# HGRN2 block products: seven levels and the diagonal in one run per unit, into two PSUM banks

## The chip, the cores and the metric

The kernel runs on one core of one Trainium2 chip. The metric is the device time of one execution in microseconds; lower is better. A core has a matrix engine (TensorE, PE in the profile, with its weight loads as PEld), a vector engine (VectorE, DVE), a scalar engine (ScalarE, ACT), a general engine (GpSimd, POOL), and SyncE (SP), whose queue issues the transfers here. The engines work from queues of their own and wait for each other through semaphores. TensorE writes its products into PSUM, of which a bank holds 512 float32 columns for 128 partitions; the other engines read them from there.

## What is computed

The reference is a decoder trunk of two layers over 1024 tokens of width 1024. Layer 0 mixes tokens with gated DeltaNet heads and a short convolution, layer 1 with HGRN2 heads and dilated sliding-window attention; a SwiGLU network follows each. The change is in the HGRN2 heads of layer 1 (four heads, key and value width 128), for which the reference says:

```python
def hgrn2_recurrence(q, k, v, log_f):
    '''S_t = diag(f_t) S_{t-1} + k_t v_t^T with k_t = 1 - f_t, o_t = S_t^T q_t, chunkwise.'''
    bcum = jnp.cumsum(lf, axis=3)
    def step(state, inp):
        q_c, k_c, v_c, b_c = inp
        decay = masked_exp(causal, b_c[:, :, :, None, :] - b_c[:, :, None, :, :])
        attn = jnp.einsum('bhtsd,bhsd->bhts', decay * q_c[:, :, :, None, :], k_c)
        o = (jnp.einsum('bhts,bhse->bhte', attn, v_c)
             + jnp.einsum('bhtd,bhde->bhte', q_c * jnp.exp(b_c), state))
        b_last = b_c[:, :, -1:, :]
        state = (state * jnp.exp(b_last[:, :, 0, :, None])
                 + jnp.einsum('bhsd,bhse->bhde', k_c * jnp.exp(b_last - b_c), v_c))
        return state, o
```

The weights of `attn` between positions t and s carry a decay for every one of the 128 key channels, so they are not one matrix product. The kernel splits the triangle of (s, t) pairs of a 128-token chunk into levels: at block size 1, 2, 4, ... 64, the pairs whose earlier position lies in the first half of a block of twice the size and whose later one lies in the second half. Within a level the decay can be written as a factor of the earlier position times a factor of the later one, both taken from the middle of the block, and the level is a matrix product of two decayed operands. The diagonal needs no decay.

## The kernel before

Tokens are held in two halves of 512. Dense products are made in three terms per tile, of a high and a low part of each operand (`mm3`, lines 125 to 137): one weight load and one matmul of up to 512 columns each. PSUM is one pool with three tags, each a rotation of banks: `psg` (two banks), `psu` (three) and `psm` (three).

In `mixer_cd`, three things are woven together. The outer order is that of the dense projections: `hgrn_v` for the values of the HGRN2 heads, `swa_v` for those of the attention, `hgrn_gates` for the output gates. Between their pieces they call `tick`, which earns credits (2.2 per unit of cost for the HGRN2 chain) and spends each on one step of `hg_chain` or of the attention's generator `local`. `chain` runs `hgrn(h, half, states)` for eight units, the two halves of heads 0 to 3; each `yield` in `hgrn` ends a step. The loop at line 1988 forces the chain on, without any projection between its steps, until three units are done, and the loop at line 2149 forces it until the unit whose gate comes next is done. Outside a block with an order written out by hand, which this stage has not, a planner orders the instructions of each engine ahead of time: by program order as the priority, taking what is ready by its own estimates. So the order of the code is a preference here, not the order that runs.

A unit's work in `hgrn`, with the lines of the code before:

- lines 2008 to 2012 load `b` (the cumulated log decay), `kk` and `q` of this unit or of the next one
- `decayed(bs)`, lines 2014 to 2032, makes the operand of one level: VectorE subtracts the reference row, ScalarE takes the exponential, VectorE multiplies with `kk` (first halves) and `q` (second halves). At block size 1, GpSimd copies `kk`. The result lies in a buffer with tag `m` (three of them) or, at sizes 8 and 64, `e4` (three, shared with later tiles of the unit)
- `blocks(od, a, x)`, lines 2034 to 2040, makes 16 products of 32 by 32 positions for one level, each with 128 rows of contraction and 32 columns of the array at a tile position; a float32 product is two matmul instructions in the trace
- the first run, lines 2048 to 2055: one `psg` bank takes the diagonal (`kk` with `q`) and levels 1, 2 and 4, 64 products, 128 instructions; VectorE masks the diagonal into `ac` and takes in each level with a masked copy (`take`, line 2043)
- the operands of levels 8, 16, 32 and 64 are made at line 2056, and two steps later comes the second run, lines 2059 to 2071: another `psg` bank, levels 8 and 16 by `blocks`, level 32 with 8 products and level 64 with 4 products of 64 columns, 88 instructions
- lines 2072 to 2081 bring both into `attn`: VectorE takes in levels 8 and 16, ScalarE copies levels 32 and 64, GpSimd copies `ac`
- lines 2084 to 2092 decay `q` and `kk` in place (`kk` for the state); line 2097 transposes `kk` into a `psg` bank; lines 2103 to 2116 update the states; lines 2118 to 2134 make and normalize the output; lines 2137 to 2142 transpose it and store it

Ten `yield`s stand in a unit. `hgrn_gates` (lines 2145 to 2157) reads the stored outputs back, makes `xg` (tag `xg`, two buffers) and stores the gated result. `out_proj` loads the mixer's outputs in `cin` tiles, in layer 1 into three buffers with tag `m`, for half 0 all eight and for half 1 two of them; the others go into other tags.

## Time and profile before

| | |
|---|---|
| time before, median of 3 runs | 2527.8 us (2527.16 to 2528.48) |
| span of the profiled execution | 2525.5 us |
| busy in the span: TensorE | 2508.2 us (99%) |
| busy: weight loads | 2086.1 us (83%) |
| busy: VectorE | 1683.2 us (67%) |
| busy: ScalarE | 1079.6 us (43%) |
| busy: GpSimd | 662.9 us (26%) |
| HBM read and written | 304.74 MB and 144.26 MB, 178 GB/s over the span |
| mean granted TensorE clock | 0.998 |

The span runs from the first to the last instruction of one profiled execution; the times of the runs are 2.3 us above it at the median. An engine's busy time is the union of its instructions' durations. Matmuls are pipelined: one starts before the last one has ended, so how close TensorE is to its limit is read from the distance between starts. An idle engine that nobody waits for costs nothing. Line numbers (L2039) are those of the kernel; a helper such as `blocks` has one line for all its callers, and is told apart by the tiles that it reads.

### The profile page before, as it was taken

How to read it: one execution, taken by the hardware profiler on the slowest of the kernel's cores; microseconds unless marked ns; L12 is line 12 of the kernel's file. 1: busy time of each engine (PE TensorE's matmuls, PEld its weight loads, DVE VectorE, ACT ScalarE, POOL GpSimd, SP SyncE). 2: the span in 40 equal slices, each digit the busy share in tenths (PEclk: the TensorE clock that was granted, in tenths of full speed). 3: DMA queues.
4: the chain of work that ended last, by engine and by line, in shares of the span. 5: the costliest groups of instructions: out<-in, count | busy, mean ns of one | idle time of the engine just before them, and what ended most of it. 6: DMA issues, size and time to landing. Idle time of an engine off the chain costs nothing. (4 is left out here: it accounts for less than half of the span.)

```text
span 2525.5 us, 37470 instructions
## 1 busy us (share of the span) xinstructions
PE 2508.2 (99%) x13955; PEld 2086.1 (83%) x13955; DVE 1683.2 (67%) x2812; ACT 1079.6 (43%) x1829; POOL 662.9 (26%) x591
## 2 busy tenths in 40 slices
PE   9999999999999999999999999999999999999998
PEld 7888888888888888887888889888888888888887
DVE  8887786685656565567788756666668565656554
ACT  5432113353333344334677535556635333334442
POOL 1321111343333300033466401000134343340001
PEclk9999999999999999999999999999999999999999
DMA  4535447325556688533444444577732555668753
GB/s 156 163 121 175 124 156 253 119 89 186 184 192 209 208 296 293 185 134 134 131 153 138 159 152 146 153 204 220 250 132 88 188 183 192 206 211 293 273 175 125
DMA packets 281454, 451.48 MB, mean 179 GB/s; under 512 B 49176, under 2 KB 137784, under 8 KB 281016
## 3 DMA queue, kind: packets, MB, share of 16 engines
q1 hardware_dynamic: 280984, 448.57, 53.3%
q8 instruction: 109, 1.79, 0.3%
q14 instruction: 73, 0.60, 0.1%
q10 hardware_dynamic: 288, 0.52, 0.1%
HBM read 304.74 MB, written 144.26 MB: 178 GB/s over the span
## 5 line engine op out<-in xcount | busy, mean ns | idle before, releaser
L103 DVE TENSOR_TENSOR w<-raw,w 128x1024 fp32r<-128x1024 f32 (+1 forms) x327 | 386.0, 1182 | 136.2 <-ACT w L102 134.3
L102 ACT CAST w<-raw 128x1024 fp32r<-128x1024 f32 (+1 forms) x327 | 309.4, 952 | 286.3 <-PE psu L137 143.2
L135 PE MATMUL psu<-hnh,w 128*128 128x512 f32 x772 | 309.0, 400 | 0.0
L137 PE MATMUL psu<-hnh,w 128*128 128x512 f32 x772 | 301.7, 391 | 0.0
L136 PE MATMUL psu<-hnl,w 128*128 128x512 f32 x772 | 301.4, 390 | 0.0
L196 POOL TENSOR_TENSOR acc<-acc,sq 128x512 f32<-128x512 f32 x52 | 78.8, 1515 | 439.4 <-ACT sq L192 435.1
L335 POOL TENSOR_TENSOR ws<-raw 128x512 f32<-128x512 f32 x54 | 70.7, 1310 | 412.2 <-DMA raw<-in_dram 317.7
L135 PEld LDWEIGHTS psu<-hnh,w 128*128 128x128 f32 x772 | 145.2, 188 | 30.8 <-ACT sq L192 0.8
L137 PEld LDWEIGHTS psu<-hnh,w 128*128 128x128 f32 x772 | 145.0, 188 | 31.1
L136 PEld LDWEIGHTS psu<-hnl,w 128*128 128x128 f32 x772 | 145.3, 188 | 28.1
L103 DVE TENSOR_TENSOR w<-ws,w 128x1024 fp32r<-128x1024 f32 x51 | 68.3, 1339 | 120.8 <-ACT w L102 120.8
L103 DVE TENSOR_TENSOR hidq<-hr,hidq 128x1024 fp32r<-128x1024 f32 x72 | 82.4, 1146 | 76.9 <-ACT hidq L102 76.8
L102 ACT CAST hidq<-hr 128x1024 fp32r<-128x1024 f32 x72 | 70.2, 979 | 102.0 <-DMA hr<-ts 59.6
L135 PE MATMUL psm<-hidq,w 128*128 128x512 f32 (+1 forms) x275 | 106.2, 386 | 0.0
L136 PE MATMUL psm<-hidq,w 128*128 128x512 f32 (+1 forms) x275 | 105.9, 385 | 0.0
L137 PE MATMUL psm<-hidq,w 128*128 128x512 f32 (+1 forms) x275 | 105.9, 385 | 0.0
L341 POOL TENSOR_TENSOR raw<-raw,ws 128x512 f32<-128x512 f32 x51 | 79.7, 1563 | 57.5 <-DVE w L103 56.2
L426 POOL TENSOR_TENSOR hid<-hid,c 128x512 f32<-128x512 f32 x44 | 62.1, 1410 | 124.1 <-ACT hid L425 123.6
L135 PE MATMUL psu<-t4h,w 128*128 128x512 f32 x240 | 93.6, 390 | 0.0
L136 PE MATMUL psu<-t4l,w 128*128 128x512 f32 x240 | 93.5, 389 | 0.0
L137 PE MATMUL psu<-t4h,w 128*128 128x512 f32 x240 | 93.5, 389 | 0.0
L137 PE MATMUL psu<-t3h,w 128*128 128x512 f32 x240 | 93.5, 389 | 0.0
(546 smaller groups left out, 6761.9 us busy)
## 6 DMA issues: line engine op xcount, KB each, us to landing
raw<-in_dram SPq DMA_DIRECT2D x225, 512.0 KB, 4.3
sd<-in_dram SPq DMA_DIRECT2D x44, 512.0 KB, 4.1
hid<-hid SPq DMA_DIRECT2D x88, 256.0 KB, 3.0
sd<-sd SPq DMA_DIRECT2D x44, 512.0 KB, 3.3
hr<-ts SPq DMA_DIRECT2D x40, 512.0 KB, 4.4
raw<-sd SPq DMA_DIRECT2D x40, 512.0 KB, 4.5
qk<-z SPq DMA_DIRECT2D x52, 256.0 KB, 3.8
hd<-h SPq DMA_DIRECT2D x48, 256.0 KB, 2.7
```

Of the source, the lines that this page charges most:

```text
L102: S.copy(hi, src)
L103: eng.tensor_tensor(lo, src, hi.bitcast(F32), op=SUB)
L135: T.matmul(o, lh, rh, start=first and i == 0, stop=False, **kw)
L136: T.matmul(o, lh, rl, start=False, stop=False, **kw)
L137: T.matmul(o, ll, rh, start=False, stop=last and i == n - 1, **kw)
L196: (eng or G).tensor_tensor(a, a, q, op=ADD)
L335: G.tensor_tensor(s[:, HT:], b[:, :HT], b[:, HT:], op=ADD)
L341: G.tensor_tensor(a[:, HT:], a[:, HT:], s[:, :HT], op=SUB)
L426: G.tensor_tensor(h, h, self.c22.pop(f), op=MULT)
```

## The change

All operands are made first, in two steps (levels 1, 2, 4; then 8, 16, 32, 64). Three `yield`s, not four, stand ahead of the products. Then one run makes all 108 products: the diagonal and levels 1, 2 and 4 into one `psg` bank, `ol`, and levels 8 to 64 into the other, `od`. All masking and copying out follows. To hold all five of its operands at once, tag `m` has five buffers in place of three; the two of `xg` are given up, and `xg` uses tag `m`. The `cin` tiles of `out_proj` in layer 1 rotate through the five as well; layer 0 keeps four.

```diff
@@ out_proj
-                f = hp.tile([P, HT], F32, tag="m", name="cin", bufs=4 - layer)
+                f = hp.tile([P, HT], F32, tag="m", name="cin", bufs=4 + layer)
@@ hgrn, decayed
-                    m = hl("m", bufs=3) if bs not in (8, 64) else hl("e4", (4, P), 3).rearrange("p c t -> p (c t)")
+                    m = hl("m", bufs=5) if bs not in (8, 64) else hl("e4", (4, P), 3).rearrange("p c t -> p (c t)")
@@ hgrn
-                ms = [decayed(1), decayed(2), decayed(4)]
+                small = [decayed(1), decayed(2), decayed(4)]
+                yield
+                ms = [decayed(8), decayed(16), decayed(32), decayed(64)]
                 yield
                 yield
                 ac = hl("ac", (4, 32))
-                od = psg()
-                blocks(od[:, 0:P], kk, q)
-                for i, m in enumerate(ms):
-                    blocks(od[:, (i + 1) * P:(i + 2) * P], m, m)
-                V.tensor_tensor(ac, c4(od[:, 0:P]), dia32[:, None, :].to_broadcast([P, 4, 32]), op=MULT)
-                for i in range(3):
-                    take(i, od[:, (i + 1) * P:(i + 2) * P])
-                ms = [decayed(8), decayed(16), decayed(32), decayed(64)]
-                yield
-                yield
+                ol = psg()
+                blocks(ol[:, 0:P], kk, q)
+                for i, m in enumerate(small):
+                    blocks(ol[:, (i + 1) * P:(i + 2) * P], m, m)
                 od = psg()
                 for i in range(2):
                     blocks(od[:, i * P:(i + 1) * P], ms[i], ms[i])
...
+                V.tensor_tensor(ac, c4(ol[:, 0:P]), dia32[:, None, :].to_broadcast([P, 4, 32]), op=MULT)
+                for i in range(3):
+                    take(i, ol[:, (i + 1) * P:(i + 2) * P])
                 for i in range(2):
                     take(i + 3, od[:, i * P:(i + 1) * P])
@@ hgrn_gates
-                        xg = hl("xg", bufs=2)
+                        xg = hl("m", bufs=5)
```

## The prediction

> **What bounds the kernel now.** I read the page's busy shares first, then the same shares of the stage that the change touches, then the waits of TensorE there, and last the timelines of TensorE and VectorE around two of the runs. A unit below is one head and half of the HGRN2 loop, numbered 0 to 7 as `chain` takes them.

> ```profile
> span 2525.5 us, 37470 instructions
> ...
> PE 2508.2 (99%) x13955; PEld 2086.1 (83%) x13955; DVE 1683.2 (67%) x2812; ACT 1079.6 (43%) x1829; POOL 662.9 (26%) x591
> ...
> PEclk9999999999999999999999999999999999999999
> ```

> TensorE is busy 99% of the span, at a granted clock that the row of slices shows at the top tenth throughout. The eight units run from about 1430 to 1810 us, and the windows of that stretch add up to the same picture:

> ```profile
> sum 380.00, PE 375.52 PEld 324.72 DVE 248.97 ACT 208.33 POOL 31.09; mean PE 93.88 PEld 81.18 DVE 62.24 ACT 52.08 POOL 7.77
> ```

> TensorE is busy 375.5 of 380 us and VectorE 249. So a gain must come from one of two places: from fewer microseconds of TensorE's own stream, or from these waits, which are all that the trace gives it in the stretch:

> ```profile
> PE psu L136 <- issue: 1.4, 1, 1.4
> PE psm L2276 <- ACT sc L2271: 1.1, 1, 1.1
> PE psu L135 <- ACT vt L1991: 0.5, 1, 0.5
> PE psg L2139 <- DVE e L2134: 0.3, 1, 0.3
> PE psm L2313 <- DVE pt L2296: 0.3, 1, 0.3
> PE psm L2241 <- DVE stat L2249: 0.2, 1, 0.2
> PE psm L2313 <- DVE dp L2284: 0.2, 1, 0.2
> ```

> They sum to 4.0 us, 0.16% of the span. A wait that VectorE, ScalarE or GpSimd loses matters only if it ends up in this list.

> **The change part by part.** First, what TensorE pays for a run by itself. This is its timeline around the first run of unit 0 (columns: start, duration, line, output and inputs, shape, count; the duration of a merged row reaches from the first start to the last end), and the durations of one block product:

> ```profile
> 1453.40 0.28 PE L136 MATMUL psu<-w,b22h 128*128 128x256 f32 x1
> 1453.52 0.28 PE L137 MATMUL psu<-w,b22l 128*128 128x256 f32 x1
> 1453.73 0.46 PE L2039 MATMUL psg<-q,kk 128*32 128x32 f32 x32
> 1454.00 1.05 PE L2039 MATMUL psg<-m 128*32 128x32 f32 x96
> 1454.98 0.39 PE L135 MATMUL psu<-w,t1h 128*128 128x256 f32 x1
> 1455.20 0.28 PE L136 MATMUL psu<-w,t1h 128*128 128x256 f32 x1
> 1455.32 0.28 PE L137 MATMUL psu<-w,t1l 128*128 128x256 f32 x1
> ...
> L2039 PE MATMUL psg<-m x1024: 189/197/216, 1454.0 to 1719.1; 128*32 128x32 f32 x171
> ```

> Read starts, not durations, since matmuls overlap. Full-array matmuls of 256 columns start every 0.12 us. The run's first product starts 0.21 us after the last of them, so going in costs 0.09. The last product ends at 1455.05 and takes 0.197, so it started at 1454.85; the next full-array matmul starts 0.13 later, where products follow each other at 0.01: going out costs 0.12. The second full-array matmul then starts 0.22 behind the first, not 0.12: another 0.10. The edges of one run are 0.09 + 0.12 + 0.10 = 0.31 us, beside 1454.85 - 1453.73 = 1.12 us for its 128 instructions.

> The change moves those 128 instructions, none fewer, to the head of the unit's second run. That run now has this form (unit 1):

> ```profile
> 1494.41 0.39 PE L137 MATMUL psu<-w,b22l 128*128 128x512 f32 x1
> 1494.72 0.46 PE L2039 MATMUL psg<-e 128*32 128x32 f32 x32
> 1495.00 0.49 PE L2039 MATMUL psg<-m 128*32 128x32 f32 x32
> 1495.34 0.45 PE L2065 MATMUL psg<-m 128*32 128x32 f32 x16
> 1495.71 0.45 PE L2070 MATMUL psg<-e 128*64 128x64 f32 x8
> 1496.09 0.66 PE L2097 MATMUL psg<-cf,kk 128*128 128x128 f32 x4
> 1496.50 0.48 PE L135 MATMUL psu<-w,t1h 128*128 128x512 f32 x1
> ```

> The two groups of 32 products take 0.28 and 0.34 us, much as the 0.27 of the first 32 in unit 0. Passing from a group of level masks to the next one, in another tile, shows no edge of 0.31, and I assume the same where the run passes from bank `ol` to bank `od`. One run's edges go per unit; the second run's own stay. That this holds for all units is seen in the windows around the eight first runs:

> ```profile
> 1453.00:1456.00 3.00, 1.32 (x128) 1.21 (x128) 1.00 1.00 347
> ...
> sum 24.00, PE 10.71 PEld 9.81; mean PE 1.34 PEld 1.23
> ```

> Eight runs of 128 instructions, 10.71 us in all, 1.32 in the first: none is split. **Removed: 8 x 0.31 = 2.5 us** of TensorE's stream. This is the term I trust.

> Second, what used to lie between the two runs. `kk` is read by the first run (its diagonal product), and overwritten at line 2092 for the transposes at line 2097. So in the kernel before, that update could be made while TensorE was still on its way to the second run:

> ```profile
> 1488.61 0.43 DVE L2023 TENSOR_TENSOR m<-b 128x256 f32<-128x256 f32 x1 [6.30 <-PE psg L2039]
> ...
> 1490.19 0.28 DVE L2053 TENSOR_TENSOR ac<-psg,cf 128x128 f32<-128x128 f32 x1
> ...
> 1490.72 0.30 DVE L2043 COPY_PREDICATED ac<-ci,psg 128x128 f32<-128x128 int32 x1
> ...
> 1492.91 0.69 DVE L2087 TENSOR_TENSOR q<-q,t 128x512 f32<-128x512 f32 x1
> ...
> 1493.85 0.68 DVE L2092 TENSOR_TENSOR kk<-kk,b 128x512 f32<-128x512 f32 x1
> ```

> In unit 1 `kk` was ready at 1494.53, before the second run began at 1494.72, and so the transposes stand right behind that run at 1496.09. They do so in two more units:

> ```profile
> 1602.88 0.45 PE L2070 MATMUL psg<-e 128*64 128x64 f32 x8
> 1603.26 0.55 PE L2097 MATMUL psg<-cf,kk 128*128 128x128 f32 x3
> ...
> 1681.49 0.45 PE L2070 MATMUL psg<-e 128*64 128x64 f32 x8
> 1681.87 0.66 PE L2097 MATMUL psg<-cf,kk 128*128 128x128 f32 x4
> ```

> With one run, the update waits for that run in every unit. VectorE then has, between the run and the transposes, the diagonal (0.28), up to five masked copies (5 x 0.30), `q` (0.69) and `kk` (0.68): 3.15 us. The transposes also need the bank of `ol` back, which the same copies free. The subtraction and exponential of `b` need no run and can stand ahead of it. Queued on VectorE behind these are the next unit's masks and the splits of weights; on TensorE nothing has to queue behind the transposes, because the planner that orders this stage can put a projection's matmuls ahead of them. By the credits of `tick`, a step leaves at least 24 matmuls of 256 columns, or 18 of 512, behind the run: 24 x 0.12 = 2.9 us or more, about the 3.15 us that are needed. What it costs where the cover falls short is bounded by nothing (as in the five units where the transposes already stand apart) and by the full 3.15 us in three units, 9.5 us. I take 0.3 us twice, the price of the nearest row, line 2139's transposes waiting on VectorE for the same kind of update: +0.6. For transposes that lose their place beside the run and now leave two more changes of shape, I take +0.1 over the three units: the row behind them, 1496.50, starts 0.41 after four transposes, so hardly an edge is seen there.

> Third, the steps. A unit yields nine times in place of ten. In the kernel before, line 1988 forces five steps of units 2 and 3 with no projection between them, among them the normalization that ends in line 2139's wait (0.3 us, above); counted through with nine steps, that loop forces only the step that closes unit 2. So -0.3. The chain ends a step or two sooner, which buys nothing: it ends long before the stage does,

> ```profile
> L2139 PE MATMUL psg<-cf,e x32: 269/272/330, 1477.7 to 1749.1; 128*128 128x128 f32 x32
> ```

> with its last transposes at 1749.1 of 1810, and TensorE's work is the same.

> Fourth, the buffers. `m` has five places, so the masks of levels 16 and 32 no longer wait for the first run:

> ```profile
> DVE m L2023 <- PE psg L2039: 23.2, 9, 6.3
> ```

> That is 23.2 us of VectorE in nine waits, 6.3 us of it the first row of the VectorE timeline above. VectorE's queue is in order, so weight splits and score reductions stood behind them; but TensorE's list shows only 0.7 us of waits on VectorE besides line 2139's (0.3 + 0.2 + 0.2). I count 0 and keep the 0.7 for the range. `xg` shares these five places, as do the `cin` tiles of `out_proj`, which had three; more loads can be under way, hidden behind a TensorE that waits for none of them in this stretch. Cost 0; if an `xg` came late, its projection would hold one of three `psu` banks. The SyncE queue carries the same transfers, none added.

> **Sum:** -2.5 + 0.6 + 0.1 - 0.3 = -2.1 us. Against the profiled execution's span that is 2525.5 - 2.1 = 2523.4; the median of the three runs, 2527.8, lies 2.3 above that span, so the forecast is 2525.7, or -0.08%. A measurement of this kernel can tell about 0.2%, 5.1 us, from no change; so this is "the same".

> **The rivals.**

> *The transposes' wait eats the gain.* The edges go, but waits of about 0.3 us appear in all eight units (2.4), or the planner keeps two runs by putting other matmuls between `ol`'s products, whose masks come first, and `od`'s. Either gives 2527.5, within a few tenths. For it: in unit 1 the update of `kk` had from 1488.61, where the first run released VectorE, to the second run at 1494.72, and loses those 6.1 us. Against it: TensorE has other matmuls to take.

> *Slower: evacuation on the path.* Both `psg` banks are taken until VectorE has emptied them, and the transposes need the first. Place: lines 2053 to 2097 in units 1, 4 and 6, where they now follow the run at once. Price: 3 x 3.15 = 9.5 us, less 2.5 and with the 0.1: +7.1, 2534.9. It decides when such waits pass 7.6 us, 2.5 in each of the three. Against it speaks the planner, and that VectorE is idle a third of the stretch (249 of 380 us busy). [...]

> *Faster.* All the 4.0 us of TensorE's waits go, since VectorE is rid of 23.2 us of waiting and every later instruction stands at another place: -2.5 - 4.0 = -6.5, 2521.3. Against it: 1.4 us of them are put down to nothing that the profile shows and 1.6 to ScalarE.

> **How the numbers follow.** The forecast (2523.5 to 2527) has 0.52; the eaten gain (2527 to 2529) 0.25; the slower rival 0.11; the faster one 0.12. The first two are within 0.2%: same 0.77, faster 0.12, slower 0.11. The range joins the first two and reaches about half way into the others: 2521.5 to 2530.5.

> **What would show it.** After the change, eight runs of 216 instructions at lines 2039 to 2070's successors, each with one pair of edges; TensorE's busy time about 2.5 us shorter; VectorE's wait of masks on block products gone; the transposes some 3 us behind the run in every unit. It is wrong if TensorE's list shows waits at the transposes, if the products stand in more than eight runs, or if the stages behind line 1288 change by more than 1 us, since a schedule that is shifted as a whole can gain or lose waits that have nothing to do with these products.

## The result: 1% slower, all of it in the stage of the eight units

The changed kernel takes 2552.0 us (median of 4 runs, 2549.3 to 2553.8) against 2527.5 us, a ratio of 1.010 with a 95% interval of 1.0087 to 1.0112. I forecast 2525.7 and a range up to 2530.5. The profiled execution has a span of 2547.5 us, 22.0 more than before. Its page looks harmless:

```profile
span 2547.5 us, 37466 instructions
...
PE 2513.0 (99%) x13955; PEld 2092.2 (82%) x13955; DVE 1686.2 (66%) x2812; ACT 1081.7 (42%) x1829; POOL 666.3 (26%) x591
```

The same number of matmuls, 99% busy as before. Windows over three stretches (columns: stretch, its length, busy time and count of each engine, granted clock, DMA share, GB/s) say where the 22 us are; first the kernel before, then the changed one:

```profile
0.00:1430.00 1430.00, 1425.51 (x6864) 1176.39 (x6864) 1005.53 (x1504) 597.32 (x926) 435.27 (x397) 1.00 0.51 171
1430.00:1808.00 378.00, 373.52 (x3896) 323.07 (x3897) 248.97 (x791) 208.33 (x552) 31.09 (x55) 1.00 0.60 183
1808.00:2525.00 717.00, 709.14 (x3198) 586.68 (x3196) 428.68 (x518) 273.93 (x352) 196.56 (x139) 1.00 0.56 192
```

```profile
0.00:1430.00 1430.00, 1424.48 (x6864) 1175.72 (x6864) 1006.73 (x1504) 597.41 (x926) 436.63 (x397) 1.00 0.52 171
1430.00:1830.00 400.00, 379.31 (x3895) 329.83 (x3896) 249.09 (x789) 208.90 (x549) 31.55 (x55) 0.98 0.56 171
1830.00:2547.00 717.00, 709.23 (x3198) 586.65 (x3196) 430.40 (x520) 275.43 (x354) 198.12 (x139) 1.00 0.57 192
```

The stretches were chosen so that the counts of matmuls agree. Ahead of 1430 us and behind the stage nothing has moved. The stage itself does 3895 matmuls in 400 us that took 378. TensorE's idle time in it has grown by 16.2 us (20.7 against 4.5) and its busy time by 5.8. The stage has lost some of its clock: 0.98 of 400 us is about 8 us of full speed that was not granted. The waits of TensorE in that stage name the rest:

```profile
PE psg L2039 <- issue: 13.8, 5, 4.6
PE psg L2066 <- issue: 2.2, 1, 2.2
PE psg L2096 <- DVE ac L2043: 1.6, 2, 0.8
PE psg L135 <- ACT hnh L102: 1.4, 1, 1.4
```

16.0 us, in six pauses, stand at the block products themselves (L2066 is the product of level 64), and the releaser is "issue": TensorE waited for no semaphore that the profile shows. The transposes' wait for VectorE, on which my slower rival was built, is the third row: 1.6 us. The timeline of the first unit shows a pause in the middle of the run:

```profile
1456.51 0.28 PE L137 MATMUL psu<-w,b22l 128*128 128x256 f32 x1
1456.72 0.46 PE L2039 MATMUL psg<-q,kk 128*32 128x32 f32 x32
...
1458.17 0.33 PE L2039 MATMUL psg<-m 128*32 128x32 f32 x14
1463.06 0.45 PE L2039 MATMUL psg<-m 128*32 128x32 f32 x17 [4.55 <-issue]
...
1464.48 0.58 PE L135 MATMUL psu<-w,t1h 128*128 128x256 f32 x1
1464.86 0.42 PE L136 MATMUL psu<-w,t1h 128*128 128x256 f32 x1
1465.07 0.41 PE L137 MATMUL psu<-w,t1l 128*128 128x256 f32 x1
```

175 matmuls go out in 1.6 us, then nothing for 4.75 us (start to start), in the midst of one level's products, whose operand is one tile that is there or not as a whole. Behind the pause the full-array matmuls start 0.21 us apart where they took 0.12: the granted clock is 0.50 in the window from 1462.80 to 1466.20 us. The windows around another pause show that by themselves:

```profile
1603.00:1607.00 4.00, 0.62 (x67) 0.52 (x58) 3.25 (x10) 1.68 (x3) 0.25 (x1) 0.89 0.89 177
1607.00:1611.00 4.00, 3.92 (x37) 3.45 (x37) 0.86 (x5) 0.66 (x3) 0.00 (x0) 0.50 0.02 7
```

What TensorE lacks is its own instructions. The table of DMA queues has two of the kind "instruction", one of them with 109 packets:

```profile
q8 instruction: 109, 1.79, 0.3%
```

1.79 MB in 109 packets is 16.4 KB each, and TensorE's 13955 matmuls and 13955 weight loads over 109 packets come to 256 instructions to a packet. The count goes with the instructions in the experiments below: 117 packets with 8 x 256 more of them, 113 with 8 x 128 more, 103 with 8 x 192 fewer. A float32 product is two weight loads and two matmuls here: the 64 products of unit 0's first run stand in the window from 1453 to 1456 us of the kernel before as 128 of each. The prediction counted the matmuls alone (128 and 88 a run); with the weight loads the runs before had 256 and 176 instructions, and the merged one has 432. In the window from 1448.5 to 1460.6 us of the changed kernel no packet of that queue moves; in the next one, 1460.6 to 1461.8, there is one (columns: queue and kind, packets, MB, share):

```profile
q1 hardware_dynamic: 160, 0.39, 84.1%
q8 instruction: 1, 0.02, 5.2%
```

By the records of the packets it starts at 1460.69 and lands at 1461.68, and TensorE goes on at 1463.06. By the same records the other five agree: TensorE goes on 1.2 to 1.5 us after a packet of that queue has landed.

**The theory, then,** is my reading of these traces: TensorE's instructions come in blocks of 256. By the starts above, a stream of full-array matmuls uses one up in an estimated 15 us or more (128 pairs of a weight load and a matmul at 0.12 us); the 128 pairs of unit 0's first run were through in 1.12 us. A run that crosses one block's edge lives on what has been brought in ahead; one that crosses two stands still until the next has come. Its rivals are my own slower case (both banks and `kk` held until VectorE is done) and the shared `m` buffers.

### The profile page after: what moved, and what is told of

The parts are those of the page before. It is cut to its first block, busy times and chain, and to the rows that moved or that the text cites. A ratio compares the mean times of both kernels' runs of the same rounds, so it can differ in the third digit from the quotient of the medians.

```text
span 2547.5 us, 37466 instructions
## 1 busy us (share of the span) xinstructions
PE 2513.0 (99%) x13955; PEld 2092.2 (82%) x13955; DVE 1686.2 (66%) x2812; ACT 1081.7 (42%) x1829; POOL 666.3 (26%) x591
## 3 DMA queue, kind: packets, MB, share of 16 engines
q8 instruction: 109, 1.79, 0.3%
## 4 chain that ended last, share of the span: by engine, by line
PE 49%; DVE 3%; issue 1%; ACT 1%; DMA 0%; SPq 0%; DVEq 0%; POOLq 0%; POOL 0%; ACTq 0%
PE psu L135 8%; PE psu L137 8%; PE psu L136 8%; PE psg L135 3%; PE psg L137 3%; PE psg L136 3%; PE psm L135 2%; PE psm L137 2%; PE psm L136 2%; PE psm L2312 1%; PE psu L130 1%; PE psu L132 1%; PE psu L129 1%; PE psg L2039 1%; PE psm L2237 0%
## 5 line engine op out<-in xcount | busy, mean ns | idle before, releaser
L102 ACT CAST w<-raw 128x1024 fp32r<-128x1024 f32 (+1 forms) x327 | 309.4, 952 | 277.0 <-PE psu L137 147.1
L135 PE MATMUL psu<-hnh,w 128*128 128x512 f32 x772 | 308.8, 400 | 0.0
L137 PE MATMUL psu<-hnh,w 128*128 128x512 f32 x772 | 301.5, 391 | 0.0
L136 PE MATMUL psu<-hnl,w 128*128 128x512 f32 x772 | 301.2, 390 | 0.0
L135 PEld LDWEIGHTS psu<-hnh,w 128*128 128x128 f32 x772 | 145.1, 188 | 31.0 <-ACT sq L192 0.8
L137 PEld LDWEIGHTS psu<-hnh,w 128*128 128x128 f32 x772 | 144.9, 188 | 31.0
L136 PEld LDWEIGHTS psu<-hnl,w 128*128 128x128 f32 x772 | 145.2, 188 | 28.2
L102 ACT CAST hidq<-hr 128x1024 fp32r<-128x1024 f32 x72 | 70.2, 979 | 104.6 <-DMA hr<-ts 64.6
L135 PE MATMUL psm<-hidq,w 128*128 128x512 f32 (+1 forms) x275 | 106.1, 386 | 0.0
L136 PE MATMUL psm<-hidq,w 128*128 128x512 f32 (+1 forms) x275 | 105.8, 385 | 0.0
L137 PE MATMUL psm<-hidq,w 128*128 128x512 f32 (+1 forms) x275 | 105.8, 385 | 0.0
L135 PE MATMUL psu<-t4h,w 128*128 128x512 f32 x240 | 93.5, 390 | 0.0
L137 PE MATMUL psu<-t4h,w 128*128 128x512 f32 x240 | 93.4, 389 | 0.0
L136 PE MATMUL psu<-t4l,w 128*128 128x512 f32 x240 | 93.4, 389 | 0.0
L137 PE MATMUL psu<-t3h,w 128*128 128x512 f32 x240 | 93.4, 389 | 0.0
```

Of the source, the lines that this page charges most:

```text
L102: S.copy(hi, src)
L135: T.matmul(o, lh, rh, start=first and i == 0, stop=False, **kw)
L136: T.matmul(o, lh, rl, start=False, stop=False, **kw)
L137: T.matmul(o, ll, rh, start=False, stop=last and i == n - 1, **kw)
```

## The experiments

**The run cut again, all else as changed.** One more step end, so that projections lie between the products into `ol` and those into `od`:

```diff
                 for i, m in enumerate(small):
                     blocks(ol[:, (i + 1) * P:(i + 2) * P], m, m)
+                yield
                 od = psg()
```

> The changed kernel with one more step end between the products into ol and those into od, so that projections lie between them again: runs of 128 and 88 matmuls (256 and 176 instructions with their weight loads); operands made first, five m buffers, xg in m and the late evacuation all stay. Theory of the instruction fetch (TensorE goes through a run faster than its instructions are brought in, 256 at a time, and the merged run crosses two such blocks): no pause over 1 us inside a run, granted clock 1.00 in the stage from 1430 us, time 2524 to 2530. Theory of the evacuation (both psg banks and kk held by the run until VectorE is done): about half of the loss stays, 2535 to 2548. Theory of the buffers (xg and cin in the five m places): 2545 to 2553, unchanged.

Measured: 2531.5 us, ratio 1.0022 (1.0013 to 1.0031), 1.5 us over the range that the fetch theory gave. Four fifths of the loss are gone. Of the rest its list of waits names 3.7 us:

```profile
PE psg L2039 <- issue: 3.7, 3, 1.8
```

Three pauses are left, in the units where the parts are nearest: two where the second part begins 4.3 and 5.0 us after the first, and unit 5, where the planner put them side by side again:

```profile
1639.91 0.46 PE L2039 MATMUL psg<-q,kk 128*32 128x32 f32 x32
1640.19 1.07 PE L2039 MATMUL psg<-m 128*32 128x32 f32 x96
1641.11 0.33 PE L2039 MATMUL psg<-e 128*32 128x32 f32 x16
1642.35 0.30 PE L2039 MATMUL psg<-e 128*32 128x32 f32 x13 [0.91 <-issue]
```

The five units whose parts lie 5.8 to 8.7 us apart have none. So the expectation "no pause" failed for a reason that fits the theory: it is the distance of the products, not a step in the code, that counts.

**The buffers alone.** The kernel before with `m` at five, `xg` in `m` and `cin` rotating through five:

```diff
-                f = hp.tile([P, HT], F32, tag="m", name="cin", bufs=4 - layer)
+                f = hp.tile([P, HT], F32, tag="m", name="cin", bufs=4 + layer)
-                    m = hl("m", bufs=3) if bs not in (8, 64) else ...
+                    m = hl("m", bufs=5) if bs not in (8, 64) else ...
-                        xg = hl("xg", bufs=2)
+                        xg = hl("m", bufs=5)
```

> The kernel before with the three edits of buffers alone (m with five, xg in m, cin rotating through five); two runs as before. Instruction fetch: 2524 to 2529. Evacuation: the same, 2524 to 2529. Buffers: 2545 to 2553.

Measured: 2527.1 us, ratio 1.0004 (0.9994 to 1.0014), no different from the kernel before within the interval. The buffers are not it. They leave one small trace, the row "PE psg L135 <- ACT hnh L102: 1.4, 1, 1.4" that the changed kernel's list of waits has above: it stands here too, and in every kernel with this edit (with 1.2 us in one of them), and in none without it. That is `out_proj` waiting for the split of a `cin` tile.

**The run made longer, nothing else.** In the kernel before, the first run's products are issued twice into the same bank:

```diff
-                blocks(od[:, 0:P], kk, q)
-                for i, m in enumerate(ms):
-                    blocks(od[:, (i + 1) * P:(i + 2) * P], m, m)
+                for _ in range(2):
+                    blocks(od[:, 0:P], kk, q)
+                    for i, m in enumerate(ms):
+                        blocks(od[:, (i + 1) * P:(i + 2) * P], m, m)
```

> The kernel before with the products of its first run issued twice into the same bank (256 matmuls, 512 instructions); nothing else is changed, no wait, operand or evacuation is added. Extra products: 8 x 1.1 = 9 us. Instruction fetch: the run crosses two blocks of 256 every time, so pauses of 0.7 to 5 us in at least six of the eight first runs, half the granted clock behind the long ones, time 2550 to 2575. Evacuation and buffers: the extra products alone, 2535 to 2539, no pause over 1 us inside a run.

Measured: 2577.6 us (one run), 52 above the 2525.9 of the kernel before beside it, of which the products themselves are 9. That is 2.6 us over the upper end of what the fetch theory gave, and 39 over its rivals'. All eight first runs pause, up to 5.9 us:

```profile
PE psg L2039 <- issue: 27.7, 8, 5.9
```

This is the plainest of the experiments: no operand, bank, buffer or wait is new, and the second half of the products needs nothing that the first had not. The eight runs of 512 instructions have pauses of 27.7 us in all, where the eight of 432 had 16.0.

**The same run with fewer instructions.** The changed kernel without the products of levels 1, 2 and 4 and their masked copies:

```diff
                 blocks(ol[:, 0:P], kk, q)
-                for i, m in enumerate(small):
-                    blocks(ol[:, (i + 1) * P:(i + 2) * P], m, m)
...
-                for i in range(3):
-                    take(i, ol[:, (i + 1) * P:(i + 2) * P])
```

> The changed kernel without the products and masked copies of levels 1, 2 and 4 (their operands are still made; the output is not the reference's): one run of 120 matmuls, 240 instructions, behind the same operands, into the same two banks. Left out: 8 x 96 matmuls at 9 ns, 7 us. Instruction fetch: no pause over 1 us inside a run, clock 1.00, 2514 to 2522. Evacuation: the update of kk still follows the run and both banks are still taken, three copies of five are gone; most of the loss stays, 2533 to 2546. Buffers: 2538 to 2546.

Measured: 2524.0 us (one run), 2 us above the upper end of what the fetch theory gave and 9 below the lower end of its nearest rival. No run has a pause; that of unit 0 goes through in 1.7 us:

```profile
1457.41 0.46 PE L2039 MATMUL psg<-q,kk 128*32 128x32 f32 x32
...
1458.69 0.45 PE L2064 MATMUL psg<-e 128*64 128x64 f32 x8
1459.08 0.39 PE L135 MATMUL psu<-w,t1h 128*128 128x256 f32 x1
```

The microseconds over the forecast stand beside waits of another kind: the state update (L2109, L2111) and `kk` (L2087) come late for TensorE. I take it that the chain's steps follow the run more closely when it has no pause; that was not taken apart.

```profile
PE psg L2118 <- DVE st L2109: 2.1, 1, 2.1
PE psg L2118 <- DVE st L2111: 1.9, 1, 1.9
...
PE psg L2092 <- DVE kk L2087: 0.8, 3, 0.4
```

**A length in between.** The kernel before with the diagonal and level 1 issued twice, 384 instructions:

```diff
+                for n in (2, 4):
+                    blocks(od[:, 0:P], kk, q)
+                    for i, m in enumerate(ms[:n - 1]):
+                        blocks(od[:, (i + 1) * P:(i + 2) * P], m, m)
```

> The kernel before with half of its first run's products issued twice (diagonal and level 1), so that the run has 192 matmuls, 384 instructions; nothing else is changed. Extra products: 8 x 64 matmuls at 9 ns, 4.6 us. Instruction fetch: between the one block of 256 that the run before crosses and the two that 512 cross; 384 instructions reach a second block's edge from half of the possible starting points, so 3 to 5 of the eight first runs pause by 0.7 us or more; 2540 to 2555. Evacuation: 2530 to 2533, no pause.

Measured: 2549.3 us (one run). Four pauses that nothing releases, as expected; but only one lies inside a run, and three just behind one, at the next thing that TensorE had to do:

```profile
PE psg L2039 <- issue: 3.9, 1, 3.9
PE psu L136 <- issue: 3.4, 1, 3.4
PE psm L2263 <- issue: 2.9, 1, 2.9
...
PE psu L135 <- issue: 1.4, 1, 1.4
```

Of the 22.5 us over the kernel before, the added products are 4.6 and the four pauses 11.6; the rest is nearly all clock, which by its record stood at half for 13.65 us.

**Where the edges fall.** This can be counted in the traces. Take TensorE's records in order of start: matmuls, weight loads and the few instructions of its queue. In the nine kernels of this document 25 of its pauses are put down to "issue" and last over 0.25 us. Each of the 25 ends at a place in this order that leaves 193 when it is divided by 256: 14529 is 56 x 256 + 193 in unit 0 of the changed kernel, 20417 is 79 x 256 + 193 behind the first run of unit 7 in the kernel before. By the theory these places are the edges of blocks; in these traces no pause of this kind ends anywhere else. The six merged runs that pause hold two such places each and stop at the second; the two that go through, units 2 and 6, hold one. Of the eight runs of 384 instructions one has its second edge inside and three have it 12 to 23 instructions behind, and there the four pauses are; the other four have no second edge so near.

Counted alike for eight first runs, the pauses inside a run and close behind one are: 240 instructions, none and none; 256 in the kernel before, none and one; 384, one and three; 432, six and none; 512, eight and one.

**The two parts further apart.** The changed kernel with two step ends in place of one between `ol` and `od`.

```diff
                     blocks(ol[:, (i + 1) * P:(i + 2) * P], m, m)
+                yield
+                yield
```

> The changed kernel with two step ends, not one, between the products into ol and those into od; one lets the planner put the two parts 4 to 5 us apart or, in one unit, side by side. Instruction fetch: the parts lie 6 us or more apart, no pause over 1 us, clock 1.00; the time is that of the kernel with the buffers alone, 2525 to 2529. Evacuation (what is left of it once the fetch is out of the way: one late evacuation, kk updated behind it): 3 us or more above the kernel before, 2529 to 2533.

Measured: 2530.9 us, ratio 1.0017 (1.0008 to 1.0026). No pause is left in any run, and the time is still 4.2 us above the 2526.8 of the kernel before beside it. So the second expectation is the one that holds for what is left, in its size: the arrangement costs some 4 us without the pauses. The largest of its waits are these:

```profile
PE psg L135 <- ACT hnh L102: 1.2, 1, 1.2
PE psm L2294 <- ACT sc L2251: 1.2, 1, 1.2
```

The first is the `cin` wait of the buffers. The others, 1.2 us and less each, are ScalarE and VectorE coming late here and there; which part of the edit causes each was not taken apart. Part of the 4 us is clock again. The profiled execution has one period of half clock, 3.41 us from 1797.51, right behind the `cin` wait and another wait for the same split; and over the eleven executions the two at a mean clock of 0.999 took 2528.6 and 2528.7 us, the four at 0.997 between 2530.5 and 2533.1.

**The edges by themselves.** The kernel before with its first run cut into two, eight more entries and exits:

```diff
                 for i, m in enumerate(ms):
+                    if i == 1:
+                        yield
+                        yield
                     blocks(od[:, (i + 1) * P:(i + 2) * P], m, m)
```

> The kernel before with its first run cut in two by two step ends (diagonal and level 1, then levels 2 and 4): three runs per unit in place of two, eight more entries and exits in all, same instructions. If the edges of a run cost the 0.31 us that I read off the timeline: 2.5 us more, 2527 to 2531, and in the trace an entry of about 0.09, an exit of about 0.12 and a late second matmul of about 0.10 us for every additional run. If runs had no edges of their own: no change. Instruction fetch: no pause, runs are shorter.

Measured: 2532.7 us, ratio 1.0022 (1.0012 to 1.0032), 3 to 8 us more, and 1.7 over the range that was given. An added run of 64 matmuls in unit 0:

```profile
1459.09 0.28 PE L137 MATMUL psu<-w,b22l 128*128 128x256 f32 x1
1459.30 0.76 PE L2039 MATMUL psg<-m 128*32 128x32 f32 x64
1459.99 0.50 PE L135 MATMUL psu<-w,hnh 128*128 128x512 f32 x1
1460.33 0.39 PE L136 MATMUL psu<-w,hnh 128*128 128x512 f32 x1
```

Going in costs 0.21 less the usual 0.12, so 0.09; the second full-array matmul starts 0.34 behind the first in place of 0.23, another 0.11. In this run the edges are as I read them. The time moved by more than their 2.5 us, and beside them stand 2.5 us of waits for the normalization of the output, where the kernel before had 0.3; the unit now has twelve steps (that these cause the waits was not shown):

```profile
PE psg L2142 <- DVE e L2137: 2.5, 3, 1.1
```

No version that makes all the products is faster than the kernel before; the one with the buffers alone is level with it.

## Why the prediction was wrong

**The step that failed** is the one on the moved instructions: "The change moves those 128 instructions, none fewer, to the head of the unit's second run", with the assumption that passing from `ol` to `od` costs nothing because the passage between groups of masks costs nothing. I priced a run as its edges plus 9 ns for each matmul, whatever its length. It has a third term, which in the changed kernel was zero in the two runs that met one block's edge and 0.7 to 4.75 us in the six that met a second one. There that term is 16.0 us of pauses by the list of waits, and some 8 us of clock, nearly all of it behind them. TensorE's busy time, which was to fall by 2.5 us, rose by 4.8 (2513.0 against 2508.2), and by 5.8 in the stage: in the main the lost clock less the edges that were saved. With the 16.2 us by which its idle time in the stage grew, that is the 22.0 us of the span. None of my rivals had this term.

**The sign was there and was read past.** "PE psu L136 <- issue: 1.4" heads the list of waits in the prediction; I counted it as something that "nothing that the profile shows" explains, and kept it for the faster rival. It stands right behind the first run of unit 7 and is this same term: the run's first edge lies 13 instructions into it and the second 14 behind its end. A packet of the instruction queue lands at 1710.90, and TensorE goes on at 1712.29, 1.4 us later.

**The edges, 2.5 us saved.** Right in kind and perhaps a little large. The added runs of the last experiment confirm about 0.31 us a run. But a merged run can have inner edges of its own. In unit 6 of the changed kernel, which has no pause:

```profile
1683.00 0.39 PE L137 MATMUL psu<-w,hnl 128*128 128x512 f32 x1
1683.32 0.46 PE L2039 MATMUL psg<-q,kk 128*32 128x32 f32 x32
...
1685.57 0.45 PE L2066 MATMUL psg<-e 128*64 128x64 f32 x8
1685.95 0.44 PE L2275 MATMUL psm<-cf,sc 128*128 128x128 f32 x2
```

From the last full-array matmul to the next thing it takes 2.95 us. Before, the two runs of that unit took 1.57 (1671.61 to 1673.18) and 1.75 (1680.12 to 1681.87), together 3.32; less one spacing of 0.23 that belongs to a full-array matmul, and with up to 0.10 for the late second one that these starts do not hold, the saving is 0.14 to 0.24 us, or 1.1 to 1.9 us for eight such units. In unit 2, the other run without a pause, the same sum gives 0.32 us (2.88 against 1.57 and 1.75, less a spacing of 0.12), which is the 0.31 of the prediction.

**The transposes behind the run, +0.6.** The two waits are there, with 1.6 us in place of 0.6, but the mechanism is not quite the one that I gave: the waits are for the masked copies that free the bank of `ol`. `kk` is updated while the run still stands in its pause, as VectorE's timeline of unit 0 shows:

```profile
1457.86 0.92 DVE L2091 TENSOR_TENSOR kk<-kk,b 128x512 f32<-128x512 f32 x1
```

It waits for the diagonal's products only, and the run lasts until 1464.5, so the cover that I thought lost was not. In all eight units `kk` is done before the run ends. The slower rival was built on 9.5 us of such waits, and they were not seen.

**The buffers at 0.** Nearly: 1.4 us in `out_proj`, where I saw only loads hidden behind TensorE.

**The steps and the rest of the arrangement, -0.3 and 0.** Wrong in sign: with the pauses taken away, 4.2 us remain over the kernel before. Some 1.7 of them are half clock in the profiled execution. The wait of VectorE's mask operands on the first run (23.2 us) is gone, as foretold. But VectorE is not rid of the wait: the update of `q` now stands in its place, in all eight units,

```profile
DVE q L2086 <- PE psg L2039: 29.9, 8, 6.1
```

and TensorE gained nothing from the exchange.

What stays open: why a block takes 2 us in one unit and 6 in another. In the changed kernel the packet started sooner where less data moved: 1.4 us after the start of the run in unit 1 (share 0.37 over its first 4 us) and 4.0 in unit 0 (0.95). Of the other four paused runs three fall into this order (just ahead of the run in unit 3, 2.2 us after its start in unit 7, 2.6 in unit 5, at shares of 0.19, 0.73 and 0.87) and unit 4 does not (2.5 us, with the largest share). That speaks for the data transfers standing in its way; it was not tried.

## What to carry to other kernels

Count the instructions of a burst, not only its time. Here TensorE went through 256 instructions in 1.12 us, and the six merged runs that paused went on with the next block 2.0 to 6.3 us after their starts. So bursts of short matmuls are to be kept to about one block, with some 6 us of long ones in between. In the two cut kernels that sufficed: parts whose starts lay 5.6 us or more apart had no pause. It is no bound, for in unit 0 of the doubled run TensorE got its next block only 7.2 us after it had passed the edge before. A wait that is put down to nothing ("issue") and stands in or behind a burst of tiny instructions is to be suspected as a shortage of instructions: all 25 of over 0.25 us in these traces ended at the edge of a block. Two bursts that look like waste may be what hides the fetch: here the kernel with two runs a unit took 2527.5 us, and that with one 2552.0.

## What the runs showed of the hardware

The longer pauses cost twice here: half the clock followed them, by the clock's record of these traces for 3.41 or 6.83 us. It did not take the longest ones. In the changed kernel the last one, 2.4 us from start to start in unit 7, has this behind it (granted clock third from the end):

```profile
1723.00:1727.00 4.00, 4.00 (x37) 3.38 (x35) 1.45 (x17) 1.81 (x9) 1.14 (x4) 0.67 0.16 46
```

And in the cut run one of 2.0 us was enough, in unit 0:

```profile
1462.10 0.27 PE L2039 MATMUL psg<-e 128*32 128x32 f32 x9 [1.81 <-issue]
```

```profile
1463.00:1467.00 4.00, 4.00 (x18) 3.20 (x17) 3.98 (x13) 2.29 (x6) 1.57 (x4) 0.57 0.78 259
```

So gaps of 2.0 and 2.4 us were followed by half clock, while one of 2.1 us in unit 1 of the changed kernel was not (granted clock 1.00 from 1498 to 1502 us): in these traces the length alone does not decide.

The clock's record shows a pattern. In the changed kernel half clock begins at 1462.79, 1606.15, 1650.52 and 1722.20 us in this stage, and these are 143.36, 44.37 and 71.68 us apart, 42, 13 and 21 times 3.4133; the two starts in the kernel before are 1368.74 us apart, 401 times that. If time is cut into stretches of that length, the pause of 2.1 us lies across a cut at 1496.92 and has 1.25 us on its longer side, while those of 2.0 and 2.4 us lie within one stretch. The nine kernels have 40 pauses of TensorE of over 1.55 us, from start to start. The 19 with 1.89 us or more inside one stretch were followed by half clock, and the 21 with 1.81 or less were not. So in these traces idle time within one stretch tells the two groups apart; this was counted, not varied by an experiment.
